# A context chain and a modulation chain trade places beside the feed-forward layers of a two-block transformer kernel

## The chip, the cores and the metric

The kernel runs on one core of a Trainium2 chip. The metric is the device time of one execution in microseconds (us); three executions of the kernel before gave 2150.39, 2150.96 and 2156.42 us, median 2150.96 us.

## What is computed

The reference takes 256 tokens of width 1024 through two blocks. The first block has two layers, each in this order: FFN1, a mixer, a cross-attention over a memory of 256 tokens, FFN2. The second block has one layer that is steered by a modulation vector and by a second sequence of 256 context tokens. Cut to what matters here:

```python
for l in range(2):                                   # first block
    x = x + 0.5 * swiglu(rms_norm(x, n1[l]), f1_in[l], f1_out[l])
    x = x + mixers(rms_norm(x, nm[l])) @ mix_out[l]
    x = x + cross_attention(rms_norm(x, nx[l]), rms_norm(mem, nk[l]))
    x = x + 0.5 * swiglu(rms_norm(x, n2[l]), f2_in[l], f2_out[l])
sh1, sc1, g1, sh2, sc2, g2 = split(silu(c) @ w_mod + b_mod, 6)      # second block
csh1, csc1 = split(silu(c_ctx) @ w_mod + b_mod, 6)[:2]
hx, hc = modulate(rms_norm(x), sh1, sc1), modulate(rms_norm(ctx), csh1, csc1)
# keys and values of hc for the attention; gated delta rule over hc -> states;
# gated delta rule over hx starts from those states
x = x + g1 * merge(attention(hx, hc), delta_rule(hx, states))
x = x + g2 * conv_ffn(modulate(rms_norm(x), sh2, sc2))
```

Two pieces of this do not depend on `x`: the modulation (it needs only `c` and `w_mod`), and the context side (it needs `ctx` and the shift and scale `csh1`, `csc1`, the first third of the modulation). They can run anywhere before the second block uses them.

## The kernel before

**Products.** Every product with a weight matrix takes the weight in loads of 512 KB into one of four buffers `raw` (line 368, queue of SyncE, SP). ScalarE (ACT) rounds a load to `wh` (three buffers, line 317), VectorE (DVE) makes the rest `wl` (three buffers, line 320), and TensorE (PE) runs three matmuls per weight tile: high times high, high times low, low times high (line 344). One FFN is 44 loads of its input matrix, taken in pairs (`gemm_pair`, line 439, 24 matmuls of 256 columns per load), and 24 loads of its output matrix (`gemm_tok`, line 396, 264 matmuls of 512 columns in all). It runs in two halves of 11 pairs and then 12 output loads (`ffn`, line 611). After each pair DVE and ACT evaluate the gate.

**The order of the work.** The kernel is traced by Python generators. Each step yields the time that it is thought to take: 2.65 units per load. `run` (line 1972) traces the main chain and, whenever the main chain has moved on, `Side.upto` (line 239) traces the steps of the side chains that are due. `turn` (line 384) lets only one chain at a time be inside a product with weights. What is left of a side chain when the main chain ends is traced at once by `drain` (line 249).

**Side chains.** `mem_kv` (line 1294) makes the keys and values of the memory. `modulation` (line 1410) has 12 chunks of four loads; each load is multiplied into an accumulator by two DVE instructions (`macc`), with no product on PE but the small ones that close a chunk; between loads it yields `dt`, and it pauses while `hold` is set, which is so during the last 12 output loads of an FFN. `context` (line 1716) loads `ctx`, norms and modulates it (`mod_norm_t`), makes its keys and values (four loads), its gates (one small load), and then runs `gdn` (line 1710): four groups of two heads, started `START[4]` units apart. A group (`gdn_group`, line 1508) has a key product of two loads, an inverse of eight 128 x 128 triangular matrices beside a value product of two loads, and a scan of two steps into the states `gS`. A flag lets an inverse start only when that of the group before is done. `inverse` (line 669) is first a forward substitution on DVE: 15 shuffles (line 694), then 15 times a product `iv_p` and a reduction `iv_x`, each of which needs the one before, then two products over 128 x 512 and two transposes (tiles `gW` and `iv_tz`); after that seven steps join the blocks with small matmuls on PE.

**Where they run.** Stages of the main chain, in order: FFN1 of layer 0, mixer 0, cross-attention 0, FFN2 of layer 0, FFN1 of layer 1, mixer 1, cross-attention 1, FFN2 of layer 1, second block. Of the side chains, memory 0 and modulation chunks 0 to 3 run beside FFN1 of layer 0, memory 1 beside cross-attention 0. The lines that place the rest (2012 to 2037):

```python
            side.put(s.now, s.modulation(Env(s, sp, (7,), "s"), 4, 12, 9.0))   # 2019
            s.run(ffn(2, 0, s.p("n1_1")), side)                                # 2020
            s.run(ffn(1, 1, s.p("nm_1")), side)                                # 2021
...
        s.run(s.mixer(1))                                                      # 2024
        cpool = ctx.enter_context(pool("cvp"))                                 # 2025
...
            side.put(s.now, s.context(Env(s, sp, (6, 7), "s")))                # 2032
            s.run(s.xattn(1, s.p("n2_1")), side)                               # 2033
            s.run(ffn(2, 1, None), side)                                       # 2034
```

The tiles that the context leaves (`gS`, `ckT`, `cv`, and the gain `knr`) are in a pool opened at line 2025. PSUM has eight banks: the FFN uses 0 to 2 for products and 3 and 4 for the rest, the cross-attention (line 1349) 0 to 2 and 3 to 5, the context 6 and 7 and, in a group outside its inverse, 3 and 4.

Of the kernel before, what the change touches and what calls it, by code (L numbers as in the profile page):

```python
# [25 lines left out]
# where the chains of a mixer start, how far apart the groups of the  # L26
# latent delta rule, where its attention starts, how far apart the groups of the context, where the side chains start
START = (7.0, 9.0, 29.0, 9.0, 30.0, 15.0, 47.0)


# ---------------------------------------------------------------- constants of the shapes
# [50 lines left out]
def _layout():  # L82
    """Columns of the array of per-partition parameters: name -> (offset, width)."""
# [114 lines left out]
def merge(*chains, flags=None):  # L198
    """Trace several chains as one: each yields the time that its next step takes, or the name of
    a flag that another chain sets; a chain (t0, generator) starts at t0."""  # L200
# [28 lines left out]
class Side:  # L229
    """Chains of work that run beside the main ones."""  # L230
# [8 lines left out]
    def upto(s, now):  # L239
        """Trace what starts up to now."""  # L240
        while s.heap and s.heap[0][0] <= now:
            t, i, g = heapq.heappop(s.heap)
            try:
                heapq.heappush(s.heap, (t + next(g), i, g))
            except StopIteration:
                pass
# [5 lines left out]
class Env:  # L252
    """A chain's own pool, PSUM banks (in turn) and names of small tiles."""
# [18 lines left out]
class Builder:  # L272
# [31 lines left out]
    # ---- short names  # L304
# [47 lines left out]
    def acc(s):  # L352
        """A bank for a product with weights."""
        s.ai += 1
        return s.bank(s.banks[s.ai % len(s.banks)])

    # ---- building blocks
# [13 lines left out]
    def sigmoid(s, out, src, bias=0.0):  # L371
        """Sigmoid of src + 2 * bias, by the tanh of the half."""
        s.act(out, src, AF.Tanh, scale=0.5, bias=bias)
        s.ts(out, out, 0.5, 0.5, OP.mult, OP.add)
# [9 lines left out]
    def turn(s):  # L384
        """Wait until no other chain's product with weights is under way."""
# [10 lines left out]
    def gemm_tok(s, w, kts, X, order=None, tail=False, at=None):  # L396
        """x (two parts, transposed) times w [128, kts * 512]: PSUM of the two token blocks."""
# [29 lines left out]
    def gemm_chan(s, w, X, o, M=128):  # L427
        """w [128, 8 * M] times x (two parts, transposed) into o [M, 256]."""
# [10 lines left out]
    def gemm_pair(s, w, i, j, X, mid=None):  # L439
        """Channel tiles i and j of w: one PSUM bank [128, 2, 256]."""  # L440
# [10 lines left out]
    def rsqrt(s, e, v, n, p=0, out=None):  # L451
        """v [P, n] in SBUF -> [P, n] of 2 ** p * v ** -0.5: a first guess, a step of Newton's kind
        with constants for that guess (to 7e-4), a step of the third order (to 1e-9)."""
# [15 lines left out]
    def squares(s, x, ss, hf):  # L469
        """Sums of squares of half hf of the columns of x [128, n, 1024] into ss [128, 2, n]."""  # L470
# [9 lines left out]
    def rstd(s, e, x):  # L480
        """Reciprocal rms of the rows of x [128, n, 1024] -> [128, n]."""
# [6 lines left out]
    # rms_norm of x in front of products: they take x times the gain, and what comes out of them  # L488
    # is scaled by the reciprocal rms of its token
    def part(s, e, x, X, g, kk):  # L490
        """Channel tiles 2 kk and 2 kk + 1 of x times the gain g [128, 8], in two parts."""
# [9 lines left out]
    def first_half(s, e, g):  # L501
        """The half of the next product's operand that the left half of s.x makes."""
# [6 lines left out]
    def mod_half(s, e, hf, sc):  # L509
        """Half hf of s.x transposed, times the channels' scales (chunk sc of s.mod), in s.xs; its squares."""  # L510
# [15 lines left out]
    def mod_rest(s, e, sh, sc):  # L526
        """modulate(rms_norm(s.x)) transposed, in two parts s.X; sh, sc: chunks of s.mod."""
# [18 lines left out]
    def second_half(s):  # L546
        """The other half, and the reciprocal rms s.nr of the rows."""
# [10 lines left out]
    def rows(s, e, R):  # L558
        """s.nr along the free axis, in all rows of R [128, 256]."""
# [5 lines left out]
    def diag_rstd(s, e, x, tmp):  # L565
        """Diagonal matrices of the reciprocal rms of the rows of x."""
# [6 lines left out]
    def scaled_t(s, e, x, dr, kk):  # L573
        """Channel tiles 2 kk and 2 kk + 1 of x, rows scaled by dr: by channel, in PSUM."""
# [7 lines left out]
    def mod_norm_t(s, e, x, X, w, sh, sc, tmp=("xn", "xm")):  # L582
        """modulate(rms_norm(x)) transposed, in two parts; sh, sc: chunks of s.mod; w: 0 latent, 1 context."""
# [11 lines left out]
    def to_chan(s, e, X, src):  # L595
        """src(tb) [128, n * 128] token-major -> X in two parts, k tiles 0.."""
# [10 lines left out]
    def row_to_all(s, out, col):  # L607
        """out [128, 128]: every row is col [128, 1] transposed."""
        s.tr(out, col.to_broadcast([128, 128]))

    # ---- FFN of the first block
    def ffn(s, wi, wo, g=None):
        """x + 0.5 * swiglu; g: the next norm's gain, where products alone follow it."""
        x, X = s.x, s.X
        s.banks = (0, 1, 2)
        with s.tc.tile_pool(name="ffn", bufs=1) as pool:
# [4 lines left out]
            def swiglu(ps, j):  # L621
                sg, th = e.t([128, 256], "sg", bufs=3), e.t([128, 256], "th", bufs=2)
                # twice silu(gate) * up, without up's rms
# [27 lines left out]
    def softplus(s, e, out, u, n):  # L651
        """max(u, 0) + log1p(exp(-|u|)) of u [128, n]; log1p(e) = 2 atanh(e / (2 + e))."""
# [15 lines left out]
    # ---- inverses of eight matrices  # L668
    def inverse(s, e, N, W, lows):
        """N = -A^T [128, 8, 128], A strictly lower (upper) triangular where lows of the half is true  # L670
        (false) -> W = (I + A)^-T. Solves the 16 x 16 blocks of the diagonal, then joins blocks."""
        nc = s.nc
        hs = [slice(0, 4), slice(4, 8)]
        # the diagonal blocks, side by side, with ones on their diagonals
# [15 lines left out]
        # row j of each block in all of the block's rows  # L690
# [5 lines left out]
        # forward substitution  # L696
# [10 lines left out]
        for hf, sl in enumerate(hs):  # L707
# [4 lines left out]
            # blocks of 32 on the diagonal alone  # L712
            nc.vector.transpose(b[:, sl], a[:, sl])
        yield 3.0
        # join blocks of 16: of every pair of blocks the columns of the one that changes
# [1340 lines left out]
```

## Time and profile before

| | us |
|---|---|
| three executions: lowest, median, highest | 2150.39, 2150.96, 2156.42 |
| profiled execution, from its first to its last instruction (the span) | 2135.9 |
| median of the executions less that span | 15.1 |
| PE busy with matmuls | 2059.1 (96% of the span) |
| PE busy with weight loads (PEld) | 1815.4 (85%) |
| DVE busy | 1603.8 (75%) |
| ACT busy | 1128.7 (53%) |
| mean granted clock of PE, as a share of 2.4 GHz | 0.965 |

The profile lists no whole time for the profiled execution beside its span; it is one execution of the same program, and what lies around the span is taken to be the 15.1 us. Times in the rows count from the start of the span. "Busy" is time with an instruction under way; matmuls overlap in the pipeline, so PE can be busy all the time and still be slow. PEclk is the granted clock as a share of full speed: 1.00 is 2.4 GHz, 0.50 is 1.2 GHz, and a value between is a stretch that had both. SPq rows are loads being issued.

### The profile page before, as it was taken

The page shows a single profiled execution, that of the slowest core. Times are in us where ns is not written, and L with a number is a line of the kernel's source. Part 1 is how long each engine was busy: PE and PEld are TensorE (multiplying, and loading weights), DVE is VectorE, ACT ScalarE, POOL GpSimd, SP SyncE. Part 2 cuts the span into 40 slices and gives each one's busy share as a digit, 9 for nine tenths or more (in the row PEclk, how much of TensorE's full clock was granted, in tenths as well). Part 3 has the DMA queues.
Part 4 walks back from the last instruction along what each step waited for, and adds up shares of the span by engine and source line. Part 5 has one row for each costly group of instructions (what it writes and reads, how often), then busy time and mean ns, then how long its engine had stood idle before and what let it go on. Part 6 is the DMA issues. An engine that isn't in the chain of part 4 may idle for free.

```text
span 2135.9 us, 37358 instructions
## 1 busy us (share of the span) xinstructions
PE 2059.1 (96%) x14344; PEld 1815.4 (85%) x14344; DVE 1603.8 (75%) x3832; ACT 1128.7 (53%) x2113; POOL 14.9 (1%) x16
## 2 busy tenths in 40 slices
PE   8999999999999999999999999999889999999998
PEld 8899887778999989888778888789778888878996
DVE  7887688577767767688577877756787887767985
ACT  6544554376445534565366455434555665546663
POOL 0000000000000000000000000000000000000000
PEclk9999999899999999999899898989998999999999
DMA  7777532145676767532134332335431122555664
GB/s 250 228 235 230 162 101 70 53 158 188 225 239 208 236 218 233 179 121 79 54 107 130 117 109 85 105 100 183 150 109 47 54 70 90 167 165 172 194 192 129
DMA packets 90570, 317.18 MB, mean 149 GB/s; under 512 B 10388, under 2 KB 12952, under 8 KB 90008
## 3 DMA queue, kind: packets, MB, share of 16 engines
q1 hardware_dynamic: 90392, 314.80, 46.0%
q8 instruction: 112, 1.84, 0.3%
q14 instruction: 66, 0.54, 0.1%
HBM read 313.72 MB, written 1.05 MB: 147 GB/s over the span
## 4 chain that ended last, share of the span: by engine, by line
PE 48%; DVE 11%; ACT 3%; issue 1%; ACTq 0%; DVEq 0%
PE b L344 46%; DVE wl L320 3%; PE b L347 2%; DVE iv_x L341 1%; DVE iv_p L320 1%; ACT wh L317 1%; DVE iv_tz L694 1%; DVE gcv L338 1%; ACT iv_c L317 1%; DVE iv_tz L320 0%; ACT sq L317 0%; DVE gW L320 0%; DVE gN L338 0%; DVE iv_n L338 0%; DVE gkd L320 0%
## 5 line engine op out<-in xcount | busy, mean ns | idle before, releaser
L317 ACT ACTIVATE wh<-raw 128x1024 fp32r<-128x1024 f32 (+2 forms) x546 | 568.7, 1042 | 550.1 <-PE b L344 444.2
L320 DVE TENSOR_TENSOR wl<-raw,wh 128x1024 fp32r<-128x1024 f32 (+2 forms) x546 | 653.3, 1201 | 209.1 <-ACT wh L317 184.7
L344 PE MATMUL b<-xTh,wh 128*128 128x256 f32 x2200 | 625.6, 285 | 4.0 <-ACT xTh L317 2.9
L344 PE MATMUL b<-xTh,wl 128*128 128x256 f32 x2200 | 622.2, 283 | 4.8 <-DVE wl L320 4.5
L344 PE MATMUL b<-xTl,wh 128*128 128x256 f32 x2200 | 623.4, 284 | 2.0 <-DVE xTl L338 1.9
L344 PEld LDWEIGHTS b<-xTh,wl 128*128 128x128 f32 x2200 | 417.9, 190 | 8.9 <-DVE wl L320 6.8
L344 PEld LDWEIGHTS b<-xTh,wh 128*128 128x128 f32 x2200 | 416.7, 190 | 9.7 <-ACT xTh L317 4.4
L344 PEld LDWEIGHTS b<-xTl,wh 128*128 128x128 f32 x2200 | 418.1, 190 | 5.4 <-DVE xTl L338 3.4
L344 PE MATMUL b<-wh,gh 128*128 128x512 f32 x440 | 175.0, 398 | 2.9 <-DVE x L338 2.8
L344 PE MATMUL b<-wl,gh 128*128 128x512 f32 x440 | 174.6, 397 | 0.3 <-DVE wl L320 0.3
L344 PE MATMUL b<-wh,gl 128*128 128x512 f32 x440 | 174.3, 396 | 0.0
L344 PE MATMUL b<-wh,xTh 128*128 128x512 f32 x400 | 163.3, 414 | 6.5 <-DVE iv_x L341 5.0
L344 PE MATMUL b<-wl,xTh 128*128 128x512 f32 x400 | 164.4, 413 | 0.3 <-DVE wl L320 0.3
L344 PE MATMUL b<-wh,xTl 128*128 128x512 f32 x400 | 162.5, 407 | 0.3 <-DVE xTl L338 0.3
L338 DVE SCALAR_TENSOR_TENSOR macc<-raw,mcs,macc 128x512 f32<-128x512 f32 x112 | 82.6, 748 | 47.8 <-DMA raw<-in_wmod_dram 47.2
L344 PEld LDWEIGHTS b<-wh,gh 128*128 128x128 f32 x440 | 83.4, 190 | 21.0 <-DVE x L338 3.3
L344 PEld LDWEIGHTS b<-wl,gh 128*128 128x128 f32 x440 | 83.2, 189 | 19.1 <-DVE wl L320 1.0
L344 PEld LDWEIGHTS b<-wh,xTh 128*128 128x128 f32 x400 | 76.4, 192 | 26.2 <-issue 9.0
L344 PEld LDWEIGHTS b<-wh,gl 128*128 128x128 f32 x440 | 83.3, 189 | 17.6
L344 PEld LDWEIGHTS b<-wl,xTh 128*128 128x128 f32 x400 | 76.9, 192 | 19.6 <-issue 3.7
L344 PEld LDWEIGHTS b<-wh,xTl 128*128 128x128 f32 x400 | 77.3, 193 | 16.4 <-issue 1.3
L317 ACT ACTIVATE iv_tz<-b 32x128 f32<-32x128 f32 (+2 forms) x96 | 31.2, 325 | 77.0 <-PE b L344 76.2
(608 smaller groups left out, 3209.7 us busy)
## 6 DMA issues: line engine op xcount, KB each, us to landing
raw<-in_f1i_dram SPq DMA_DIRECT2D x88, 512.0 KB, 4.4
raw<-in_f2i_dram SPq DMA_DIRECT2D x88, 512.0 KB, 4.0
raw<-in_wmod_dram SPq DMA_DIRECT2D x48, 512.0 KB, 4.4
raw<-in_wup_dram SPq DMA_DIRECT2D x44, 512.0 KB, 4.3
raw<-in_f1o_dram SPq DMA_DIRECT2D x40, 512.0 KB, 4.3
raw<-in_f2o_dram SPq DMA_DIRECT2D x40, 512.0 KB, 4.3
raw<-in_wi_q_dram SPq DMA_DIRECT2D x40, 512.0 KB, 3.7
raw<-in_wi_a_dram SPq DMA_DIRECT2D x32, 512.0 KB, 3.6
```

The source lines that it names most:

```text
L317: return s.nc.scalar.activation(out, in_, func, scale=scale, bias=bias, **kw)
L320: return s.nc.vector.tensor_tensor(out, a, b, op=op)
L338: return s.nc.vector.scalar_tensor_tensor(out, a, sc, b, op0=op0, op1=op1)
L341: s.nc.vector.tensor_reduce(out, in_, axis=AX.X, op=op)
L344: s.last_mm = s.nc.tensor.matmul(out, lhsT, rhs, start=start, stop=stop).ins
L347: s.nc.tensor.transpose(out, in_, s.c("ident"))
L694: nc.vector.stream_shuffle(AR[:, j, :, j:], NC[:, :, j:], [j] * 16 + [16 + j] * 16)
```

## The change

The modulation of chunks 4 to 11 leaves FFN2 of layer 0 and FFN1 of layer 1, and runs beside cross-attention 1 and FFN2 of layer 1, with 6.5 units between loads where it had 9. The context runs where the modulation was. Its groups start 80 units apart where they started 30 apart, and outside its inverses it uses PSUM banks 5 and 4. The pool of its results opens before mixer 1, so these 12.5 KB per partition are held through that mixer. The program is built with a smaller scratch area for dynamic DMA. The diff also takes out docstrings and comments; without those it is:

```diff
-START = (7.0, 9.0, 29.0, 9.0, 30.0, 15.0, 47.0)
+START = (7.0, 9.0, 29.0, 9.0, 80.0, 15.0, 47.0)
...
     def context(s, e):
...
-        yield from s.gdn(e, e.on((3, 4)), X, False, s.S)
+        yield from s.gdn(e, e.on((5, 4)), X, False, s.S)
...
         s.run(s.mixer(0))
+        cpool = ctx.enter_context(pool("cvp"))
+        s.S = cpool.tile([128, 2, 8, 128], F32, name="gS")
+        s.ckv = (cpool.tile([128, 2, 256], F32, name="ckT"), cpool.tile([128, 2, 256], F32, name="cv"))
+        s.knr = cpool.tile([128, 128], F32, name="knr")
+        s.nc.sync.dma_start(s.knr, d["kn"].to_broadcast([128, 128]))
         with pool("side") as sp:
             side = Side()
             side.put(s.now, s.mem_kv(Env(s, sp, (6, 7), "s"), 1))
...
-            side.put(s.now, s.modulation(Env(s, sp, (7,), "s"), 4, 12, 9.0))
-            s.run(ffn(2, 0, s.p("n1_1")), side)
-            s.run(ffn(1, 1, s.p("nm_1")), side)
+            side.put(s.now, s.context(Env(s, sp, (6, 7), "s")))
+            s.run(s.ffn(d["f2i_0"], d["f2o_0"], s.p("n1_1")), side)
+            s.run(s.ffn(d["f1i_1"], d["f1o_1"], s.p("nm_1")), side)
             s.hold = False
             side.drain()
         s.run(s.mixer(1))
-        cpool = ctx.enter_context(pool("cvp"))
-        s.S = cpool.tile([128, 2, 8, 128], F32, name="gS")
-        s.ckv = (cpool.tile([128, 2, 256], F32, name="ckT"), cpool.tile([128, 2, 256], F32, name="cv"))
-        s.knr = cpool.tile([128, 128], F32, name="knr")
-        s.nc.sync.dma_start(s.knr, d["kn"].to_broadcast([128, 128]))
         with pool("side") as sp:
             side = Side()
-            side.put(s.now, s.context(Env(s, sp, (6, 7), "s")))
+            side.put(s.now, s.modulation(Env(s, sp, (7,), "s"), 4, 12, 6.5))
             s.run(s.xattn(1, s.p("n2_1")), side)
-            s.run(ffn(2, 1, None), side)
+            s.run(s.ffn(d["f2i_1"], d["f2o_1"], None), side)
...
-    nc = _bacc.Bacc("TRN2", target_bir_lowering=False, num_devices=1)
+    nc = _bacc.Bacc("TRN2", target_bir_lowering=False, num_devices=1, dynamic_dma_scratch_size=2048)
```

## Rows read from the trace of the kernel before

**Rows 1.** The page: busy time by engine, and the granted clock in 40 slices.

```profile
PE 2059.1 (96%) x14344; PEld 1815.4 (85%) x14344; DVE 1603.8 (75%) x3832; ACT 1128.7 (53%) x2113; POOL 14.9 (1%) x16
...
PEclk9999999899999999999899898989998999999999
```

**Rows 2.** Timeline of the SP queue: start, length, loads; the first load of each stage.

```profile
487.94 6.80 SPq L368 DMA_DIRECT2D raw<-in_f2i_dram x3
...
683.02 0.33 SPq L368 DMA_DIRECT2D raw<-in_f1i_dram x1
...
877.09 0.33 SPq L368 DMA_DIRECT2D raw<-in_mic_dram x1
...
1064.32 23.27 SPq L368 DMA_DIRECT2D raw<-in_xq_dram x3
...
1150.91 10.57 SPq L368 DMA_DIRECT2D raw<-in_f2i_dram x4
...
1498.58 0.33 SPq L368 DMA_DIRECT2D raw<-in_axial_dram x1
```

**Rows 3.** Busy time by stretch: length, PE, PEld, DVE, ACT, POOL, PEclk, DMA share, GB/s.

```profile
485.00:683.00 198.00, 194.66 (x1393) 180.96 (x1392) 146.75 (x230) 97.92 (x142) 0.00 (x0) 1.00 0.67 220
683.00:877.00 194.00, 190.34 (x1379) 177.97 (x1378) 140.62 (x218) 91.57 (x130) 0.00 (x0) 0.99 0.68 220
1064.00:1151.00 87.00, 84.16 (x483) 65.96 (x483) 64.32 (x182) 54.91 (x127) 0.00 (x0) 1.00 0.36 117
1151.00:1498.00 347.00, 332.56 (x2545) 304.65 (x2544) 250.42 (x687) 173.45 (x363) 0.00 (x0) 0.90 0.37 118
```

**Rows 4.** Busy time by stretch around the context's inverses, columns as in rows 3.

```profile
1200.00:1210.00 10.00, 8.14 (x69) 7.76 (x67) 10.00 (x27) 5.81 (x15) 0.00 (x0) 1.00 0.54 176
...
1200.00:1250.00 50.00, 46.63 (x379) 43.16 (x378) 32.14 (x113) 25.49 (x64) 0.00 (x0) 0.80 0.21 68
1250.00:1300.00 50.00, 47.17 (x385) 43.93 (x385) 34.84 (x86) 21.07 (x47) 0.00 (x0) 0.80 0.39 127
...
1343.00:1380.00 37.00, 36.56 (x289) 30.23 (x289) 23.17 (x89) 18.76 (x45) 0.00 (x0) 0.86 0.25 73
1380.00:1440.00 60.00, 57.80 (x427) 52.23 (x426) 37.63 (x78) 23.60 (x45) 0.00 (x0) 0.83 0.36 117
...
1397.00:1422.00 25.00, 23.87 (x193) 21.16 (x191) 10.28 (x17) 6.68 (x19) 0.00 (x0) 0.59 0.26 86
1430.00:1480.00 50.00, 50.00 (x427) 50.00 (x426) 35.47 (x56) 23.79 (x35) 0.00 (x0) 1.00 0.56 178
```

**Rows 5.** The chain of waits, 1060 to 1500: start, length, engine and tile.

```profile
1210.61 22.00 PE b L344 x167
...
1396.39 1.03 DVE gW L320
```

**Rows 6.** Costliest DVE groups, 1182 to 1212.1, beside the first inverse: busy us, mean ns.

```profile
L320 DVE TENSOR_TENSOR wl<-raw,wh 128x1024 fp32r<-128x1024 f32 x9 | 10.9, 1216 | 0.1
L341 DVE TENSOR_REDUCE iv_x<-iv_p 128x8 f32<-128x16 f32 (+14 forms) x15 | 4.2, 283 | 0.0
L320 DVE TENSOR_TENSOR iv_p<-iv_tz,iv_x 128x16 f32<-128x16 f32 (+14 forms) x15 | 4.1, 272 | 0.1
L694 DVE STREAM_SHUFFLE iv_tz<-iv_n 128x128 f32<-128x128 f32 (+14 forms) x15 | 2.4, 258 | 0.0
L338 DVE SCALAR_TENSOR_TENSOR gcv<-b,prm,gcv 128x255 f32<-128x255 f32 x4 | 1.9, 481 | 0.0
```

**Rows 7.** Groups of the context inside cross-attention 1, 1098.6 to 1158.

```profile
L344 PE MATMUL b<-sXh,wh 128*128 128x256 f32 (+1 forms) x24 | 7.2, 298 | 0.0
...
L344 PE MATMUL b<-wh,sXl 128*128 128x512 f32 x16 | 6.3, 395 | 0.0
...
L344 PE MATMUL b<-gcv,iv_tz 128*128 128x128 f32 x32 | 4.1, 275 | 0.0
```

**Rows 8.** Waits in FFN2 of layer 0, 485 to 683: total us, times, longest.

```profile
DVE macc L338 <- DMA raw<-in_wmod_dram: 24.6, 12, 3.7
```

## Prediction

> **What bounds the kernel now.** I read the page first. PE has a matmul under way for 96% of the span, at a mean granted clock of 0.965 [rows 1], so the time is PE's, and what is left is in places where PE is starved or its clock is down. To find them I took the order of the SP queue, which says when each stage's first load is issued [rows 2], and from it the busy time by stage [rows 3]. From first load to first load, FFN2 of layer 0 takes 683.0 - 487.9 = 195.1 us, FFN1 of layer 1 takes 877.1 - 683.0 = 194.1, cross-attention 1 takes 1150.9 - 1064.3 = 86.6, and FFN2 of layer 1 takes 1498.6 - 1150.9 = 347.7. The four are 823.5 us, and everything the change moves lies in them. The first two FFNs carry the modulation and run at a clock of 1.00 and 0.99. The last carries the context, at 0.90 [rows 3].
>
> The finer windows say why [rows 4]. Around the first inverse DVE is busy for all of 1200 to 1210 and PE issues 69 matmuls; later, with the FFN alone, it is 427 in 50 us, or 85 in 10. Then the clock goes to its lower level, 1.2 GHz: 0.80 is the mean of 1200 to 1250. The chain of waits says the same: when the forward substitution has ended, the chain is PE from 1210.6 on for 22 us [rows 5]. There are four such places, one per group, the last after the `gW` product at 1396.4. So beside the context, DVE and PE take turns at being the bound: DVE starves PE, the clock falls, and then a slow PE leaves DVE idle.
>
> The windows with a clock under 1.00 give what that costs: (1 - clock) times length is 10.0 + 10.0 + 5.2 + 10.2 = 35.4 us [rows 4]. PE has no matmul for another 347.0 - 332.6 = 14.4 us [rows 3]. Together that is 50 us, 12.5 for each group.
>
> **The change, step by step.** The sum is made on the profiled execution, whose span is 2135.9; the median is 15.1 above it, and I carry that over.
>
> *The schedule.* One FFN is 68 loads of 2.65 units, 180 units; the context adds 20 larger loads, 53 units. Two FFNs with the context are thus some 413 units. Its first group starts about 50 units in (norm 12, keys and values 26, gates 12), the last 240 later, and one group takes about 64 units: the end is near 354, and nothing is left to drain.
>
> *FFN2 of layer 0 and FFN1 of layer 1 lose the modulation.* At the pace of 427 matmuls in 50 us [rows 4] the 1056 matmuls of 256 columns take 123.7 us; the 24 output loads take the rest, which I bound by the 194.6 us mean of the two stages as they are. In them DVE stood at the head of its queue for the modulation's loads for 24.6 us in one FFN [rows 8], and PE had no matmul for 198.0 - 194.7 = 3.3 and 194.0 - 190.3 = 3.7 us [rows 3]. Taking those away gives about 191. I take 190; the ends are 187 (twice the pause as well) and 194.6 (nothing back).
>
> *They gain the context.* Beside FFN2 of layer 1 its price was 347.7 - 190 = 157.7 us, of which 50 were the losses above; 107 is work. Inside cross-attention 1 it put 48 matmuls of 512 columns, 72 of 256 and 32 of 128 [rows 7], where one row stands for each of three like ones and the 128 have one. At the pace above a matmul of 256 columns takes 0.117 us; doubled or, for the 128, kept as an upper bound, this is 11.2 + 8.4 + 3.7 = 23.3, and with the gates' small ones 24. So 131 us of work move.
>
> *What the spreading saves* is the uncertain term. Beside the first inverse DVE did, in 30 us, some 15 us of the inverse (4.2 + 4.1 + 2.4, the two products, two transposes and the start, 4.2), 17 of the FFN and of value loads, and about 6 for the next group's key product: four `gcv` of 1.9 us, 0.7, some 1 of a square root, two of the nine `wl`, 2.4 [rows 6]. The FFN steps that the trace puts there are 14.4 units, about 15.6 us of PE. So DVE overran PE by some 14 us, and 6 of these are the neighbour's. At 80 units the neighbour is gone, the inverse itself is not. Ends: all 50 us saved, or none. I take a little under half: two of four falls of the clock remain (20 us), and half the pauses (7), 27 in all.
>
> The sum for the two FFNs is 2 x 190 + 131 + 27 = 538 us, where they took 389.2.
>
> *Cross-attention 1 loses the context and gains modulation.* 24 us of matmuls go. They filled waits, though: in 87 us PE was without a matmul for only 2.8 [rows 3]. From the product of the queries to that of the values lies a chain of transposes, scores, a softmax and transposes back, each waiting for the one before; I estimate that half of the 24 us comes back as waiting. Ends: none (62.6) or all (86.6). I take 75. Here the clock stayed at 1.00 [rows 3]; now the only matmuls left in the waits are the scores and transposes themselves. The Trainium skill (Perfetto Trace Analysis, Matmul Optimizations) says that TensorE scales its power with its use, so matmuls should run back to back in batches. By that the clock falls here, and the stage gives nothing back; that is rival D.
>
> *FFN2 of layer 1 gains modulation.* The nearest rows are the two FFNs that carried it: 194.6 us. The spacing is now 6.5: 59 units of cross-attention and 180 - 32 of the FFN (the last 32 are held) are 207, and 32 loads need 208. So about 23 of them fall into one FFN, where 16 did; 7 more at two DVE instructions each, mostly beside PE, I put at 2 us, and a load or two drained behind the FFN at 2 more. 199, with ends of 194.6 and 205.
>
> *Taken as nothing.* Banks 5 and 4: the FFN uses 3 and 4 only at its start and end. The earlier load of `knr` and the held pool issue nothing else. The smaller scratch: every load is on a hardware queue, and the trace shows no wait for it; if that is wrong, loads would be issued late, with no row for a price.
>
> **The sum:** 538 + 75 + 199 = 812 us where it was 823.5, so 11.5 less: 2150.96 - 11.5 = 2139.5, rounded to **2139**. PE's matmuls are the same in number, so all of this is loss that goes or comes.
>
> A second view of the gain: weight loads keep PE busy 304.7 of 347 us, 87.8%, beside the context and 181.0 of 198, 91.4%, beside the modulation [rows 3]. The Trainium skill (Perfetto Trace Analysis, Identifying the Most-Contended Engine) takes that share, and not matmul busy time, for the distance to the limit. By it I estimate that bringing the context's stage up to the other gives 347 x (1 - 0.878/0.914) = 14 us at most, where the sum without it allows 50.
>
> **The rivals.**
>
> *A, the forecast, 0.42.* Half the loss stays: 2139.
>
> *B, the burst is gone, 0.15.* With 80 units between groups DVE is never far enough behind, no clock falls, some 7 us of pauses stay. 20 us less: 2119. For it: on average DVE is busy no more beside the context (250 of 347 us) than beside the modulation (147 of 198) [rows 3], so spread evenly it would fit. Against it: the last group, with no key product behind it, had a clock of 0.59 in 1397 to 1422 all the same [rows 4].
>
> *C, each group costs what it did, 0.26.* The inverse alone is the cause: each of four forward substitutions starves PE and is followed by 20 us at 1.2 GHz, now in FFN2 of layer 0 and FFN1 of layer 1. The 50 us stay, 23 more than in the sum, while cross-attention 1 has given its filling away: 823.5 + 11.5, **2162**, slower. It decides from 39 us of loss upwards. For it: that same last group.
>
> *D, cross-attention runs slow, 0.12.* Its waits are empty, the clock falls there and the next FFN starts at 1.2 GHz: nothing saved, 86.6 where I have 75, so 2151.
>
> *E, the change does not do what it says, 0.05.* The modulation does not fit beside its new stages, or the context's products wait for their turn so long that groups are not apart. Drained loads cost about 6 us more than A: 2145.
>
> **How the numbers follow.** About 0.3%, 6.5 us, can be told from no change. A is faster for 0.36 of its 0.42 and within the bound for 0.06; B is faster; C slower for 0.20, the same for 0.06; D the same for 0.07, slower for 0.05; E faster 0.02, the same 0.01, slower 0.02. That gives faster 0.53, same 0.20, slower 0.27. The range goes from 2106 (B with cross-attention's lower end) to 2168 (C with the FFN's upper end). A's own range is 2128 to 2152.
>
> **What would show it.** In the stages of FFN2 of layer 0 and FFN1 of layer 1: first load to first load 538 us together, and the granted clock by windows. Two falls of 20 us are A, none B, four C. The four `gW` products should lie some 100 us apart, all before the first load of mixer 1. Cross-attention 1 should be near 75 us at a clock mostly 1.00, FFN2 of layer 1 near 199 without a `gcv` in it. I am wrong if the two FFNs take over 550 us or under 520, or if mixer 1 or the second block, which the change leaves alone, differ by more than 5 us.

## The result, and the profile after

The changed kernel takes 2178.3 us (median of 4 runs, 2172.8 to 2182.2), beside 2151.6 for the kernel before on the same chip: a ratio of 1.0116, with an interval of 1.0069 to 1.0162. It is 27 us, or 1.2%, slower. I had forecast 2139 and a range that ended at 2168, so the sign was wrong and the range did not hold the time.

The profiled execution has a span of 2174.8 us and was timed at 2176.5, so 1.7 us lie around a span. The 15.1 us that I had carried over from the kernel before were therefore something else: if as little lies around that span, that execution was some 13 us faster than the median. In the later comparisons 66 runs of the kernel before lay between 2128 and 2165. Differences of a few us between single profiles say nothing; this is why the stages are read below by what is lost in them, and the verdicts by medians.

The timeline of the SP queue in the changed kernel, first load of each stage (start, length, what is loaded), answers to [rows 2]:

```profile
491.65 3.21 SPq L368 DMA_DIRECT2D raw<-in_f2i_dram  x2
...
790.13 2.99 SPq L368 DMA_DIRECT2D raw<-in_f1i_dram  x2
...
1063.74 0.33 SPq L368 DMA_DIRECT2D raw<-in_mic_dram  x1
...
1250.95 0.33 SPq L368 DMA_DIRECT2D raw<-in_wmod_dram  x1
...
1309.30 0.33 SPq L368 DMA_DIRECT2D raw<-in_f2i_dram  x1
...
1531.45 0.33 SPq L368 DMA_DIRECT2D raw<-in_axial_dram  x1
```

Cross-attention 1 now opens with a load of the modulation, at 1250.95. The stages take 298.5 and 273.6 us (FFN2 of layer 0, FFN1 of layer 1), 58.3 (cross-attention 1) and 222.2 (FFN2 of layer 1). These four are 852.6 us, where they were 823.4 (823.5 in the prediction, by rounding): 29.2 more. Mixer 1 takes 187.2 in both. The first stages (3.7) and the second block (6.0) make up the rest of the 38.9 us between the two profiles.

The busy time by stage answers to [rows 3] (length; PE, PEld, DVE, ACT, POOL with counts; PEclk; DMA share; GB/s):

```profile
491.00:790.00 299.00, 292.67 (x2141) 264.92 (x2140) 217.28 (x523) 155.44 (x298) 0.00 (x0) 0.95 0.45 141
790.00:1063.00 273.00, 265.77 (x1938) 247.22 (x1937) 186.67 (x433) 131.01 (x240) 0.00 (x0) 0.90 0.44 139
...
1251.00:1309.00 58.00, 51.17 (x289) 38.00 (x289) 44.27 (x104) 32.83 (x72) 0.00 (x0) 0.99 0.49 158
1309.00:1531.00 222.00, 207.30 (x1429) 190.86 (x1430) 156.18 (x261) 99.93 (x154) 0.00 (x0) 0.95 0.65 211
```

I call the **loss** of a stretch its length less PE's busy time, plus (1 - PEclk) times its length; what is left is **work**. The table gives the two terms in this order. The second term is good to half a hundredth of the length, 1 to 3 us.

| | early pair: FFN2 of layer 0, FFN1 of layer 1 | late pair: cross-attention 1, FFN2 of layer 1 | loss of both | work of both |
|---|---|---|---|---|
| before [rows 3] | 7.0 + 1.9 = 8.9 | 17.3 + 34.7 = 52.0 | 60.9 | 826 - 61 = 765 |
| changed | 13.6 + 42.2 = 55.8 | 21.5 + 11.7 = 33.2 | 89.0 | 852 - 89 = 763 |

The work is the same, and the loss has grown by 28 us. The early pair, which lost 9 with the modulation, loses 56 with the context. The late pair got only 19 of its 52 back.

What the early pair loses lies at the same places as before. Windows of the changed kernel around the `gW` product, the first of the two products that end a substitution, of the first (635.8), second (752.7) and fourth group (979.4), columns as above:

```profile
625.00:638.00 13.00, 11.09 (x47) 8.29 (x45) 12.66 (x25) 4.48 (x6) 0.00 (x0) 1.00 0.56 182
638.00:666.00 28.00, 27.95 (x179) 22.04 (x180) 6.85 (x12) 7.49 (x21) 0.00 (x0) 0.51 0.20 63
746.00:760.00 14.00, 12.03 (x94) 10.81 (x93) 12.57 (x26) 5.46 (x9) 0.00 (x0) 1.00 0.42 120
...
969.00:983.00 14.00, 11.85 (x102) 11.68 (x101) 13.83 (x32) 5.97 (x9) 0.00 (x0) 1.00 0.51 171
983.00:1010.00 27.00, 27.00 (x195) 24.59 (x195) 8.44 (x15) 8.60 (x23) 0.00 (x0) 0.50 0.21 60
```

In the first and the fourth group DVE is busy for nearly all of 13 or 14 us, PE is without a matmul for 2, and then the clock is at 1.2 GHz for 27 us with DVE mostly idle. I call such a stretch at 1.2 GHz a **fall**. The third group does the same from 864 on, for 24 us. The second was spared in this execution: PE stood for 2 us there too, and the clock stayed at 2.4 GHz. The groups are now 107 to 120 us apart, and each shows this by itself.

The chain of waits, 975 to 1015, shows how a substitution ends:

```profile
979.02 0.33 DVE iv_x L341
...
979.38 1.07 DVE gW L320
980.44 0.99 DVE iv_tz L320
...
981.56 33.50 PE b L344 x244
```

The last sum of the substitution, then the two products that spread the diagonal blocks, `gW` and `iv_tz`, and then PE alone. PE stood for these two. The list of what PE waited for in the early pair (us in total, times, longest) says so:

```profile
PE b L344 <- DVE iv_tz L320: 8.2, 4, 2.3
```

Four waits of 2 us, at the inverse's first joining products. In the last FFN of the kernel before the same wait was half as long:

```profile
PE b L344 <- DVE iv_tz L320: 4.4, 4, 1.2
```

### The profile page after: what moved, and what is told of

Its sections match the earlier page's. It is cut to its first block, busy times and chain, and to the rows that moved or that the text cites. A ratio compares the mean times of both kernels' runs of the same rounds, so it can differ in the third digit from the quotient of the medians.

```text
span 2174.8 us, 37356 instructions
## 1 busy us (share of the span) xinstructions
PE 2084.0 (96%) x14344; PEld 1836.3 (84%) x14344; DVE 1605.2 (74%) x3832; ACT 1129.3 (52%) x2113; POOL 14.9 (1%) x16
## 4 chain that ended last, share of the span: by engine, by line
PE 74%; DVE 16%; DMA 4%; ACT 4%; issue 2%; SPq 0%; DVEq 0%; ACTq 0%
PE b L344 71%; DVE wl L320 5%; DMA raw<-in_wmod_dram 4%; PE b L347 3%; ACT wh L317 1%; DVE iv_x L341 1%; DVE iv_tz L694 1%; DVE macc L338 1%; DVE iv_p L320 1%; DVE gcv L338 1%; DVE sg L320 1%; ACT iv_c L317 0%; DVE iv_tz L320 0%; ACT sq L317 0%; DVE sg L338 0%
## 5 line engine op out<-in xcount | busy, mean ns | idle before, releaser
L317 ACT ACTIVATE wh<-raw 128x1024 fp32r<-128x1024 f32 (+1 forms) x546 | 568.8, 1042 | 561.0 <-PE b L344 437.6
L320 DVE TENSOR_TENSOR wl<-raw,wh 128x1024 fp32r<-128x1024 f32 (+1 forms) x546 | 654.4, 1205 | 232.4 <-ACT wh L317 204.4
L344 PE MATMUL b<-xTh,wl 128*128 128x256 f32 x2200 | 629.5, 287 | 8.6 <-DVE wl L320 7.4
L344 PE MATMUL b<-xTh,wh 128*128 128x256 f32 x2200 | 632.7, 288 | 3.4 <-ACT xTh L317 2.4
L344 PEld LDWEIGHTS b<-xTh,wl 128*128 128x128 f32 x2200 | 423.3, 193 | 12.3 <-DVE wl L320 8.9
L344 PEld LDWEIGHTS b<-xTh,wh 128*128 128x128 f32 x2200 | 422.1, 192 | 8.9 <-ACT xTh L317 4.0
L344 PEld LDWEIGHTS b<-xTl,wh 128*128 128x128 f32 x2200 | 423.0, 192 | 3.3 <-DVE xTl L338 1.0
L344 PEld LDWEIGHTS b<-wh,xTl 128*128 128x128 f32 x400 | 77.2, 193 | 15.6 <-issue 1.0
```

The lines of the kernel that those rows point to most:

```text
L317: return s.nc.scalar.activation(out, in_, func, scale=scale, bias=bias, **kw)
L320: return s.nc.vector.tensor_tensor(out, a, b, op=op)
L344: s.last_mm = s.nc.tensor.matmul(out, lhsT, rhs, start=start, stop=stop).ins
```

## The experiments

What each run did to the loss comes from its windows over the early and the late pair, one profile each. The windows of the late pair start at the last load of mixer 1; counted so, the pair took 435.9 us in the kernel before and 282.1 in the changed kernel. Times are medians, ratios are to the kernel before in the same comparison.

### Is it the distance of the groups, or the burst in each?

**The distance undone.**

```diff
-START = (7.0, 9.0, 29.0, 9.0, 80.0, 15.0, 47.0)
+START = (7.0, 9.0, 29.0, 9.0, 30.0, 15.0, 47.0)
```

> The changed kernel with one number undone: the groups of the context start 30 units apart again, not 80, and stay beside FFN2 of layer 0 and FFN1 of layer 1. Theory I (the burst is inside a group: each inverse starves TensorE by itself, whatever its distance to the next): within 6 us of the changed kernel, 2172 to 2184, with three or four falls of the clock of 20 to 27 us, now mostly in FFN2 of layer 0. Theory II (the spreading does harm: a neighbour's products used to fill the waits of an inverse, and a group by itself leaves them empty): 15 us less or more, 2163 or below, and the falls shorter. Theory III (the spreading helps as I forecast, and the loss is elsewhere): 2190 or above.

2174.3 us, ratio 1.0147 (1.0106 to 1.0188): no different from the changed kernel. Windows of FFN2 of layer 0 and FFN1 of layer 1:

```profile
497.00:887.00 390.00, 377.05 (x2739) 341.36 (x2738) 278.76 (x772) 195.00 (x408) 0.00 (x0) 0.88 0.35 116
887.00:1072.00 185.00, 184.80 (x1341) 173.98 (x1340) 124.10 (x184) 90.27 (x130) 0.00 (x0) 1.00 0.58 188
```

The whole context now lies in one FFN, with a loss of 13.0 + 46.8 = 59.8 us (three falls of 24 to 27 us and one of 10), and the other FFN runs bare, with no side chain beside it, in 185 us with PE idle for 0.2. Together 575, where the changed kernel has 572. Spreading the groups saved nothing, and did no harm either: theories II and III fall.

**The forward substitution left out.** In the context's inverses the 15 products and sums are not done, so the inverse is not one.

```diff
-        for i in range(1, 16):
+        for i in range(1, 16 if not skip else 1):
```

> The changed kernel with the 15 steps of the forward substitution (15 products and 15 sums on VectorE) left out of the context's four inverses, which leaves the rest of each inverse, its matmuls too, as they are. Theory I (VectorE's burst starves TensorE, and the clock falls for that): the falls beside the context, 27.3 + 23.9 + 27.3 us at half clock or 39 us of time, go for the most part; 2178 - 39 = about 2140, and some us less for the pauses. Rival (the falls come from the small matmuls that join the blocks after the substitution): three falls stay, and the time drops by less than 12 us, 2166 or above.

2137.4 us, ratio 0.9972 (0.9946 to 0.9998); 37 us less than the run above, in the same comparison. The early pair:

```profile
498.00:1028.00 530.00, 525.05 (x4076) 486.95 (x4076) 380.31 (x834) 284.45 (x537) 0.00 (x0) 0.98 0.46 151
```

PE issues as many matmuls, 4076, the small ones that join the blocks among them. The loss is 5.0 + 10.6 = 15.6 us, with two short falls of 7 and 10 us left, and the wait for `iv_tz` L320 is gone. So it is VectorE's burst that costs, not the small matmuls after it. The edit takes out a little more than the 15 steps: the planner's seven pauses between them go too, and `gW`, which then has nothing to wait for, is done 87 us or more earlier.

**The burst spread inside the group.** No work is added or left out; the planner only counts more for the steps. `fine` is true for the context's inverse alone.

```diff
             nc.vector.stream_shuffle(AR[:, j, :, j:], NC[:, :, j:], [j] * 16 + [16 + j] * 16)
+            if fine and j % 5 == 4:
+                yield 2.0
...
-            if i % 2 == 0:
+            if fine or i % 2 == 0:
                 yield 1.2
...
             nc.vector.transpose(b[:, sl], a[:, sl])
+            if fine and hf == 0:
+                yield 2.0
```

> The changed kernel with the burst spread inside a group: in the context's inverse the planner counts 1.2 units for each step of the forward substitution and not for two, the shuffles go in three lots of 2 units, and the two halves of the diagonal blocks are 2 units apart. Nothing else changes, and no work is added. Theory I: the falls beside the context get rarer or shorter; by half, 20 us less, about 2158; all gone, about 2138. Theory II or the small matmuls as the cause: three falls as before, 2172 to 2184.

2148.4 us, ratio 1.0012 (0.9972 to 1.0051): nothing is left of the slowdown that can be told, by a few yields. The early pair, and what PE still waited for in it:

```profile
496.00:1042.00 546.00, 531.84 (x4078) 491.92 (x4077) 405.09 (x955) 286.32 (x537) 0.00 (x0) 0.97 0.45 147
```

```profile
PE b L344 <- DVE iv_tz L320: 4.8, 2, 2.9
PE b L344 <- DVE iv_tz L715: 4.6, 2, 2.6
```

The loss is 14.2 + 16.4 = 30.6 us, near the 27 that I had let stay after the spreading between groups. The waits at the joining products are as long as ever; the falls after them are shorter, 3 to 14 us for each group. The profiled execution took 2168.2 us, 20 above the median: mixer 1, whose code is the same, took 197 us to its last load where the changed kernel's took 186, with a fall of 27 us that is not there in the changed kernel's profile.

**More FFN work ahead of the joining products**, first alone, then with the pace.

```diff
-        yield 3.0
+        yield 10.0 if fine else 3.0
 
         odd = lambda ap, hf: ...
```

> The changed kernel with 10 units in place of 3 between the diagonal blocks and the first joining products of the context's inverse, so that more of the FFN's products stand ahead of them in TensorE's queue. Theory V (TensorE, in order, waits at the joining products for VectorE, which is behind by the burst): the wait of 1.8 to 2.9 us at the end of a substitution shrinks below 1, and the falls beside the context go from 85 us of half clock to under 40; 2178 less 20 or more, below 2160. Rival (the burst before the hole does it): the falls stay, 2170 to 2185.

> The changed kernel with the pace of the earlier paced run and this lead of 10 units. Theory V: the falls beside the context that the pace left, 31 us of half clock, go too, and the pauses halve: 2148 less 10 to 25, 2123 to 2138. If the place itself is worse for another reason: it stays above the paced kernel before, 2120, by 20 or more.

Alone it does nothing that can be told: 2170.8 us, ratio 1.0137 (1.0066 to 1.0209), with four falls of 20 to 27 us and the wait unchanged:

```profile
PE b L344 <- DVE iv_tz L320: 8.8, 4, 2.6
```

The trace of its first group shows why: PE goes from an FFN product that starts at 632.53 straight to the first joining product at 634.67, with 1.76 us of waiting between, as in the changed kernel (1.77). No more FFN products came to stand ahead, and the next `wl`, which they would need, is made on DVE only at 635.66, behind `gW` and the transposes. With the pace it takes 2130.1 us, ratio 0.9929 (0.9899 to 0.9960). The early pair, and the windows of its first group (`gW` at 636.5):

```profile
491.00:1016.00 525.00, 516.70 (x4073) 479.31 (x4073) 402.93 (x954) 286.73 (x535) 0.00 (x0) 1.00 0.47 153
```

```profile
625.00:638.00 13.00, 12.85 (x57) 10.19 (x56) 12.69 (x24) 4.88 (x5) 0.00 (x0) 1.00 0.53 174
638.00:666.00 28.00, 28.00 (x288) 25.91 (x287) 17.19 (x27) 14.21 (x29) 0.00 (x0) 1.00 0.44 147
```

The wait for `iv_tz` L320 is no longer in the list, none of the four groups is followed by a fall, and the loss of the early pair is 8.3 us. In 638 to 666 PE issues 288 matmuls where the changed kernel issued 179. So the mechanism is this: DVE falls behind in the burst, PE comes to the joining products early and stands, the clock falls in most groups, and a slow PE pays it back for 20 to 27 us. Whether the thinner feed before the stand or the stand itself brings the fall is not separated: with the pace alone the stands were as long and the falls shorter, and in the changed kernel's second group a stand had no fall behind it.

**The banks.**

```diff
-        yield from s.gdn(e, e.on((5, 4)), X, False, s.S)
+        yield from s.gdn(e, e.on((3, 4)), X, False, s.S)
```

> The changed kernel with the context's small products on the PSUM banks 3 and 4 again, not 5 and 4. My step, banks cost nothing: 2172 to 2184. Rival (banks hold the FFN's joints or the context up): 8 us or more to either side.

2174.2 us, ratio 1.0145 (1.0102 to 1.0188): nothing. In that profile all four groups have a fall, of 20 to 27 us.

### What do the two moves cost by themselves?

**The context alone moved.** The later modulation is back beside the early pair, next to the context, on PSUM bank 3 and with 10 units between loads.

```diff
             side.put(s.now, s.context(Env(s, sp, (6, 7), "s")))
+            side.put(s.now, s.modulation(Env(s, sp, (3,), "s"), 4, 12, 10.0))
...
-            side.put(s.now, s.modulation(Env(s, sp, (7,), "s"), 4, 12, 6.5))
```

> The changed kernel with the later modulation back beside FFN2 of layer 0 and FFN1 of layer 1, one load per 10 units, next to the context; cross-attention 1 and the last FFN run bare. If it is the modulation that costs beside cross-attention 1 and the last FFN: these two stages, 282 us from the last load of mixer 1 on, become 55 + 187 = 242 or less, with no fall of 20 us, and the two earlier FFNs grow from 572 by at most 20, to 592: about 2158 in all. If the empty waits of cross-attention 1 are the cost: the fall of 20 us stays, the two stages take 260 or more, and the total stays above 2170.

2179.1 us, ratio 1.0162 (1.0113 to 1.0212). Early and late pair:

```profile
494.00:1094.00 600.00, 576.02 (x4128) 525.36 (x4127) 439.10 (x1022) 284.76 (x533) 0.00 (x0) 0.91 0.49 161
...
1280.00:1535.00 255.00, 246.56 (x1663) 218.59 (x1662) 166.20 (x292) 130.83 (x225) 0.00 (x0) 0.99 0.47 154
```

The late pair runs bare in 255.8 us with a loss of 8.4 + 2.6 = 11.0. So cross-attention's empty waits cost little; with the modulation beside it the pair takes 282.1 and loses 33. But the early pair grows by 28, more than I had expected. The modulation costs 26 us in the late pair and 28 beside the context in the early one.

**The modulation alone moved**, next to the context in its old place, on PSUM bank 5 and with the change's scratch area; the early pair runs bare.

```diff
-            side.put(s.now, s.modulation(Env(s, sp, (7,), "s"), 4, 12, 9.0))
...
             side.put(s.now, s.context(Env(s, sp, (6, 7), "s")))
+            side.put(s.now, s.modulation(Env(s, sp, (5,), "s"), 4, 12, 6.5))
```

> The kernel before with the later modulation alone moved to cross-attention 1 and the last FFN, next to the context that is there, at 6.5 units each; FFN2 of layer 0 and FFN1 of layer 1 run bare. The bare pair takes 369 to 372 us where it took 389. If the modulation costs 20 to 27 us wherever it is: within 10 us of the kernel before. If VectorE, with context and modulation, is overrun in the one FFN: 20 us or more above it, 2166 or more.

2174.2 us, ratio 1.0132 (1.0067 to 1.0198). Early and late pair:

```profile
496.00:874.00 378.00, 377.68 (x2706) 352.79 (x2705) 253.17 (x376) 185.91 (x271) 0.00 (x0) 1.00 0.56 184
...
1060.00:1528.00 468.00, 433.50 (x3104) 388.90 (x3103) 354.29 (x947) 230.21 (x493) 0.00 (x0) 0.91 0.44 146
```

The early pair gets 11 us of its 389 back, where I had expected 17 to 20, and the late pair, with 34.5 + 42.1 = 76.6 us of loss, takes 32 more (467.7 for 435.9). Either move alone costs what both together cost: 1.0132 and 1.0162 against 1.0116, with intervals that overlap. The price is not a sum of two moves. Only the arrangement of the kernel before avoids it among these four.

The two bare pairs, 377.9 and 255.8 us, give each chain its price by place. The modulation costs 389.2 - 377.9 = 11 us in its old place and 282.1 - 255.8 = 26 in its new one, 15 more. The context costs 435.9 - 255.8 = 180 in its old place and 572.1 - 377.9 = 194 in its new one, 14 more. These two make up the 29 us by which the four stages grew (in their sum the bare pairs drop out). Each is from single profiles: with the late pair of the scratch run below, 419 us, the context's 14 would be 31.

**The modulation later.**

```diff
-            side.put(s.now, s.modulation(Env(s, sp, (7,), "s"), 4, 12, 6.5))
             s.run(s.xattn(1, s.p("n2_1")), side)
+            side.put(s.now, s.modulation(Env(s, sp, (7,), "s"), 4, 12, 4.7))
```

> The changed kernel with the later modulation started only when cross-attention 1 is over, 32 loads at 4.7 units each beside the last FFN, so that cross-attention 1 runs bare. If the modulation itself holds cross-attention 1 up (12 us of TensorE waiting behind its sums on VectorE, 5 for a load of the output weights): cross-attention 1 with its end gets 10 to 15 us shorter, the last FFN at most 5 longer, 2165 to 2172. If the empty waits are the cause: its fall of the clock of 20 us stays, and the time is within 6 us of 2178, or above it where the denser modulation holds the last FFN up.

2171.6 us, ratio 1.0152 (1.0101 to 1.0203). The late pair takes 277.1 us where it took 282.1, with a loss of 23.6. In place of its fall of 20 us cross-attention 1 has two here, of 7 and 3, so that fall went with the modulation and not with the empty waits; a gain in the total cannot be told.

**Matmuls added that nobody reads**, 108 of 512 columns, put in at cross-attention 1 or 20 units into the last FFN.

```diff
+        for i in range(27):
+            ps = s.bank(6)
+            for j in range(4):
+                s.mm(ps, dm[:, :128], dm)
+            yield 2.0
...
+            side.put(s.now, s.filler(Env(s, sp, (6,), "s")))
             s.run(s.xattn(1, s.p("n2_1")), side)
```

> The changed kernel with 108 matmuls of 512 columns added whose product nobody reads, 4 per 2 units, from the start of cross-attention 1 on; at 45 in 10 us of a full FFN that is 24 us of TensorE, the amount that the context had there. Theory IV (cross-attention 1 has waits that matmuls can use and a modulation can't, while an FFN by itself has none: TensorE was without a matmul for 0.2 of 185 us in the run with spacing 30): the two stages from the last load of mixer 1 on, 282 us, grow by at most 10, the fall of 20 us there goes, and the time is 2168 to 2186. Rival (no slack there): 24 us more, 2195 or above.

> The same 108 matmuls at the same pace, from 20 units after the start of the last FFN on instead. Theory IV: paid in full, 20 to 28 us more than the changed kernel, 2198 to 2206, and 15 us or more above the run with them in cross-attention 1. Rival (place does not matter): within 8 us of that run.

2180.0 us, ratio 1.0149 (1.0098 to 1.0200), and 2176.1, ratio 1.0161 (1.0114 to 1.0208). The late pair in the one and in the other:

```profile
1246.00:1535.00 289.00, 281.25 (x1842) 246.80 (x1841) 204.30 (x369) 135.53 (x228) 0.00 (x0) 0.99 0.58 195
```

```profile
1263.00:1545.00 282.00, 278.84 (x1839) 243.82 (x1839) 203.25 (x370) 133.57 (x228) 0.00 (x0) 1.00 0.60 199
```

The pair takes 288.6 and 282.2 us where it took 282.1, so the filler lengthens it by 6.5 and by nothing, and its loss falls from 33 to 10.6 and 3.2. I had counted the filler as 24 us; by the work in these windows it is some 30. The second run did not separate the two places: half of its filler ran before 1337, at the end of cross-attention 1, nearly all the rest after 1406. What both show is that some 30 us of TensorE lie unused in the late pair with the modulation. At the end of cross-attention 1, the changed kernel and the run with the filler there:

```profile
1305.00:1331.00 26.00, 15.38 (x50) 11.43 (x51) 13.64 (x38) 8.65 (x23) 0.00 (x0) 0.61 0.44 143
```

```profile
1302.00:1328.00 26.00, 25.37 (x127) 19.91 (x127) 17.26 (x46) 12.31 (x28) 0.00 (x0) 1.00 0.41 143
```

Without the filler PE stands for 10.6 of 26 us and the clock is down for most of them; with it the clock stays at 2.4 GHz. One wait alone is 6.1 us long, from 1303.2 to 1309.3: the product that PE issues next is the modulation's, and the sum `macc` that it needs is queued on DVE among the making of `wl` and the steps of norms. The list of PE's waits in 1251 to 1331 of the changed kernel has it first:

```profile
PE b L344 <- DVE macc L338: 6.1, 1, 6.1
```

**The context after cross-attention 1**, in the kernel before, with its groups 20 units apart so that it ends with the last FFN.

```diff
-            side.put(s.now, s.context(Env(s, sp, (6, 7), "s")))
             s.run(s.xattn(1, s.p("n2_1")), side)
+            side.put(s.now, s.context(Env(s, sp, (6, 7), "s")))
```

> The kernel before with its context started when cross-attention 1 is over, so that it lies beside the last FFN alone, its groups 20 units apart so that it ends with it; the modulation stays beside the earlier FFNs. Theory IV (the loss of the change is that the context leaves cross-attention 1): cross-attention 1 and the last FFN take 450 to 460 us where they took 436, and the time is 2165 to 2180, most of what the whole change costs. Rival (the two earlier FFNs are a worse place for another reason): 2140 to 2158, as before.

2153.1 us, ratio 1.0032 (0.9996 to 1.0068). Theory IV does not hold in the form that I gave it: the context does not have to lie in cross-attention 1, and leaving it explains some 7 of the 27 us, 15 at the upper end of the interval and nothing at the lower.

**The scratch area** of the change in the kernel before.

> The kernel before with the smaller DMA scratch alone. All theories: within 0.3% of the kernel before, and the stages 195, 194, 187, 87 and 348 us as there, but for falls of the clock that come and go. Rival (the scratch holds loads up): FFN stages longer by 3 us or more each.

2149.1 us, ratio 1.0031 (0.9990 to 1.0072), and the early pair takes 391 us. It costs nothing that can be told, 15 us at the upper end of the interval. The profile shows the spread of one schedule: the late pair loses 34 us here and lost 52 in [rows 3], while mixer 1, the same in both, took 12 us longer here.

### A version that beats both

The pace in the kernel before; the same with the pace in every inverse of the kernel; and pace and lead in the kernel before.

> The kernel before, with its context and modulation where they were, and the burst spread inside a group as in the paced run of the changed kernel. The paced run got 26 us of the two FFNs (572 to 546 us) with the falls beside the context from 85 to 31 us. Theory I: the last FFN, 347.7 us with 71.7 us at half clock, gets 15 to 30 us shorter, and the time is 0.985 to 0.993 of the kernel before, the fastest of all. Rival (there the groups overlap, and the longer ones are drained behind the FFN): no gain, 0.997 to 1.005.

> As the run above, and the same pace in the inverses of the mixers and of the second block, where the kernel before has falls of 17, 17 and 31 us at half clock. Theory I taken further: up to 20 us less than the run above, 0.975 to 0.988. Rival (there the inverse is on the path that sets the end, and little other work waits for VectorE): no gain or a loss against the run above.

> The kernel before with the pace and the lead of 10 units. There the paced run had a single fall of 3.4 us beside the context and holes of 0 to 0.6 us at the end of a substitution, so there is nothing left for the lead: 2112 to 2128, or a little longer, since the groups get 7 units longer and the last may drain behind the FFN.

| | us | ratio | interval |
|---|---|---|---|
| before, context paced | 2120.5 | 0.9878 | 0.9839 to 0.9918 |
| before, all inverses paced | 2116.0 | 0.9851 | 0.9813 to 0.9888 |
| before, context paced, with the lead | 2120.8 | 0.9892 | 0.9833 to 0.9950 |

The late pair of the first:

```profile
1073.00:1472.00 399.00, 384.60 (x3030) 343.64 (x3030) 317.39 (x870) 227.71 (x488) 0.00 (x0) 1.00 0.39 129
```

Its loss is 14.4 us where it was 52, at the work that it had. The three cannot be told apart. Pacing the other inverses adds nothing that is certain, and the lead nothing, as expected.

## Why the prediction was wrong, by its steps

*What bounds the kernel* was right, and so was the sentence that all of it is loss that goes or comes: the work of the four stages was 762 to 771 us in every arrangement that kept the whole context in them and added nothing.

*What the spreading saves* is the step that failed. I had taken 23 of 50 us as saved and let 27 stay, since 6 of the 14 us by which DVE overran PE were the neighbour's. The runs showed that the inverse's own burst is enough, at 30 units as at 80: the early pair lost 56 us, none of the 50 was saved. The two FFNs took 572 where the sum had 538; the loss explains 29 of these 34 us, and the work, 516 where I had 511, the rest. The evidence was in the prediction itself: the last group in [rows 4] had no key product behind it and a clock of 0.59 all the same. I had quoted that for rival C and given it 0.26. The 14 us were not a measure of what PE loses, either. The parts of 15, 17 and 6 us add up to 38 in a stretch of 30.1 us, 1182 to 1212.1, in which DVE was busy for 30.0, and PE had a matmul under way for 27.5 of it. The term for the two bare FFNs, 2 x 190, held: they took 377.9 us in the run with the modulation alone moved.

*Cross-attention 1 and the last FFN* together: 280.5 measured, 274 forecast. The split, 75 and 199, was wrong (58 and 222), because the FFN's first loads are issued while cross-attention's chain still runs; only the sum means something. The reason was right in part. The stage does lose its clock, as rival D had it, and the filler there cost 6.5 us or less; but the bare pair loses only 11 us, so it is the modulation among those waits that hurts, in DVE's queue. At its end cross-attention 1 has a fall of 20 us with the modulation, and without it two of 3 us, in the run with the context alone moved. The Trainium skill (Perfetto Trace Analysis, Matmul Optimizations) asks for matmuls back to back because power scales with use; the two windows above agree with it, 0.61 without the filler and 1.00 with it.

*The rivals* were priced as if one excluded the other. C (each group costs what it did) and D (cross-attention runs slow) are in different stages, and both came. My own prices for the two together, 23 + 12 on 2139, give 2174; the measurement is 2178, and the range ended at 2168. That 2174 comes so near is in part luck, since D's 12 us were for empty waits and not for the modulation in them.

*The banks* and *the scratch* cost nothing that can be told, as I had taken them. The held pool was not run by itself; mixer 1, through which it is held, took 187.2 us in both profiles.

*The second view* did not help. The share of weight loads beside the context rose to (264.9 + 247.2) / 572 = 89.5%, where it was 87.8%, while the loss beside the context went from 49 to 56 us. The Trainium skill (Perfetto Trace Analysis, Identifying the Most-Contended Engine) judges TensorE's distance to the limit by that share, among others; by it these stages would have come nearer to the limit. One reason is in the trace: in the early pair a weight load of the FFN's input products takes 331 ns where the clock is at 1.2 GHz and 188 at 2.4, so a fall raises the share.

*The 15.1 us* carried over were no constant; they did not decide the sign.

*The signs of being wrong* that I had named came twice: the two FFNs took over 550 us, and the second block differed by 6.0, over 5. The second block's difference is the clock's: its mean was 0.960 where it was 0.969, which is 6.3 us of its length.

**What stays open.** Unpaced, the context loses more in its new place (54 to 66 us in seven profiles) than in the old one (34, 39 and 52 in three). The wait at the joining products is about 2 us there; in the old place it is 1.1 in two profiles and 1.8 in the third, where the context starts after cross-attention 1. Where it is gone, so is the difference in loss beside the context: 8 us in the new place, 14 in the old. Why it is longer there was not found; neither the banks nor the distance of the groups changes it.

## What to carry to other kernels

When side work starves the bounding engine, look at how many of its steps the plan issues at once, before moving it or spreading it by whole groups: here a few yields inside one routine were worth some 26 us in either kernel, and 50 units more between the groups nothing. A side chain can cost little beside one kind of stage and much beside another: the modulation cost 11 us beside two bare FFNs and 26 to 32 elsewhere, so its old place was worth keeping. A work item that is moved leaves a stage whose waits it may have filled, and takes its own burst along; these are two separate losses that can both come, so a forecast should price them together. And compare a single profile with the spread of the runs before taking any constant from it.

## What was not expected of the hardware

The clock's falls differ between executions of one schedule: near 306 us, in the first mixer, six of the eighteen profiles have one of 20 to 24 us and the others, that of before among them, have none. Where it is, FFN2 of layer 0 starts at 496 to 498 us and not at 485 to 494. One of the eighteen, with all inverses paced, ran other code there, and it is not among the six. A starved PE at 2.4 GHz followed by 20 to 27 us at 1.2 GHz costs some 12 us for a wait of 2. Neither half of the cure sufficed alone: the lead without the pace left every fall whole, the pace alone shortened them, and both together left none after an inverse. And some 30 us of useless matmuls cost nothing in the total that can be told: they ran where PE had stood, and the clock stayed up.
